# Zero matmuls on TensorE ahead of the first slabs, and the second chunk's split two squares earlier

## The chip, the cores and the metric

One core of a Trainium2 chip runs the whole kernel. Its engines work side by side, each through its own queue in order: TensorE (PE: matmuls and transposes; PEld is its weight load), VectorE (DVE), ScalarE (ACT), GpSimd (POOL) and SyncE (SP, which here issues nearly all transfers). The metric is the device time of one execution in microseconds (us), lower is better.

## What is computed

One layer of a diffusion model's trunk on 1024 tokens of width 1024, with 256 context tokens. Cut to what matters here:

```python
m = silu(cond) @ w_ada + b_ada                 # cond: c for x, c_ctx for ctx
shift, scale, gate = split(m, 3)
h  = rmsnorm(x, norm_g) * (1 + scale) + shift  # (1024, 1024); likewise hc from ctx
q, k, v, za, u, bg, cg, zc = split(h @ w_in)   # w_in: 1024 x 4096
attn = neighbourhood_attention(...) * silu(za)
conv = bg * conv3(cg * u) * silu(zc)
out  = x + gate * (concat(attn, conv) @ w_out)
```

All of it is float32. The large matmuls get that precision from operands split in two: a high part rounded to TensorE's faster format (fp32r), and a low part, the rest. Three products (high·high, high·low, low·high) make one.

## The kernel before

The change lies in the first 35 us, the opening of the kernel. There, h has to be made before the projections can run, and it is made in column blocks k = 0 to 7 of 128 channels, each in two halves (512 tokens each): `turn(half, k)` writes the high part `hh[k]` and the low part `hl[k]` from transposed tiles of x.

What is needed for that, by the names in the code (line numbers are those of the kernel before):

- **Slabs.** `load_slab(m, j)` fetches 256 columns of `w_ada`, for shift (j = 0) or scale (j = 1), 1024 KB each; (0, 0) and (0, 1) come in two halves of 512 KB. `products(m, j)` (line 594) multiplies them on TensorE by the two conditioning vectors `c2` (silu of c and c_ctx); `row_copy(m)` takes the result out of PSUM on ScalarE, and `modulation(m, rw)` turns it into columns with eight small matmuls, and adds bias and norm gain on VectorE (tile `ab`). m = 0 serves k = 0 and 1, m = 1 serves k = 2 and 3, and so on.
- **x.** Eight tiles of 128 tokens, `xx[0]` to `xx[7]`, 512 KB each. For tile n, `square(xx[n], n)` sums its squares on ScalarE, `root(n)` adds epsilon on VectorE and takes the power -0.5 on GpSimd, and `norm(xx[n], n)` scales the tile on VectorE. `transposed(half, k)` then transposes the four tiles of a half on TensorE, and `turn` applies `ab`: the high part on ScalarE, the same value in float32 on VectorE or ScalarE, and the difference on VectorE.
- **Chunks.** `chunk_load(CU, k)` fetches three blocks of 128 columns of `w_in` for channels k (192 KB, tile `wr`); `split_chunk(k)` makes `wh` on ScalarE and then `wl` on VectorE. `first_columns(half, k)` (line 670) is nine matmuls of 512 columns into the six accumulators `acc0`: three with `wh` and the high part of h, three with `wl` and the high part, three with `wh` and the low part.

Loads are issued on SP in the order slabs (0, 0) and (0, 1); x's tiles 0 to 3; chunk 0; x's tiles 4 to 7; chunk 1; slabs (1, 0) and (1, 1); chunks 2 and 3; slab (2, 0). Later slabs wait for the tile of an earlier one to come free.

The order of all this is written out by hand. The class `ordered` (line 44) chains the instructions of each engine in the order in which the program text emits them, so what stands first in the text runs first on its engine, and an instruction that waits holds up all behind it on the same engine. The text of the opening is:

```python
 718    products(0, 0)
 ...
 742    first_columns(0, 0)
 743    square(xx[6], 6)
 744    norm(xx[5], 5)
 745    root(6)
 746    square(xx[7], 7)
 747    norm(xx[6], 6)
 748    root(7)
 749    split_chunk(1)
 750    norm(xx[7], 7)
 751    first_columns(0, 1)
 752    products(1, 0, range(4))
 753    transposed(1, 0)
 754    turn(1, 0, act)
 755    products(1, 0, range(4, KT))
```

Before line 718, and ahead of everything else on TensorE, stands one transpose that brings the small vectors (c, c_ctx, norm gain, biases) into columns (`pv`, line 561). After the opening come the projections to q, k, v (with their own norms and rotations), the attention over 32 quarter heads with the gate and convolution projections as fillers, and the output projection.

Nearly every instruction goes through one helper line, so the profile shows L55 for most of them; they are told apart by tile names. In the profile, `tr` is the PSUM tile of transposes, products and modulation, `acc` the accumulators of first_columns, `c` the tile of `c2`, `xss` the sums of squares, `sqj` the squares.

Of the kernel before, what the change touches and what calls it, by code (L numbers as in the profile page):

```python
# [12 lines left out]
BF16 = mybir.dt.bfloat16  # L13
# [6 lines left out]
P = 128  # L20
# [19 lines left out]
def body(tc, es, x, ctxt, w_ada, b_ada, w_in, q_g, k_g, rpbr, w_out, vecs, cst, out):  # L40
# [21 lines left out]
    pe, act, dve, pool = every = [ordered(e) for e in (nc.tensor, nc.scalar, nc.vector, nc.gpsimd)]  # L62
    sp = ordered(nc.sync)

    def sbuf(name, side=None, bufs=1):
        kw = {} if side is None else {"side": side}
        return tc.tile_pool(name=name, bufs=bufs, reuse_waits="tile", **kw)
# [83 lines left out]
    cvp = hs.enter_context(sbuf("cvp", side="right"))  # L151
# [14 lines left out]
    def chunk_split(raw):  # L166
        raw = raw[:].rearrange("p a b -> p (a b)")
        wh = wpp.tile([P, 384], F32R, name="wh", tag="wh", bufs=12)
        wl = wpp.tile([P, 384], F32R, name="wl", tag="wl", bufs=12)
        act.copy(wh, raw)  # L170
        dve.tensor_tensor(wl, raw, wh[:].bitcast(F32), ALU.subtract)
        return wh, wl
# [348 lines left out]
    def tr():  # L521
        return ps0.tile([P, 512], F32, name="tr", tag="tr", bufs=2)

    strict[:] = every + [sp]
    xx, slabs, highs, lows, chunks, mods, pts = {}, {}, {}, {}, {}, {}, {}
# [31 lines left out]
    acc0 = [{}, {}, {}]  # L557
    for u, half in (0, 0), (2, 0), (0, 1), (2, 1), (1, 0), (1, 1):
        acc0[u][half] = ps0.tile([P, 512], F32, name=f"acc{u}{half}", tag=f"acc{u}{half}")

    pv = tr()
    pe.transpose(pv[:, :nvec], vec[:nvec], ident[:nvec, :nvec])
    dve.tensor_copy(vecT, pv[:, :nvec])
# [1 line left out]
    dve.tensor_scalar(b1, bsc, 1.0, None, ALU.add)  # L565
    c4 = cp.tile([P, KT, 4], F32R, name="c4")
    act.copy(c4[:, :, 0:2], c2)
    dve.tensor_tensor(c4[:, :, 2:4], c2, c4[:, :, 0:2].bitcast(F32), ALU.subtract)

    sums = {}  # L570

    def square(xtile, n):

        sqj = cvp.tile([P, D], BF16, name="sqj", tag="cu", bufs=1)
        sums[n] = xp.tile([P, 1], F32, name="xss", tag="xss", bufs=4)
        act.activation(sqj, xtile, AF.Square, scale=1.0 / 32, accum_out=sums[n])

    def root(n):
        dve.tensor_scalar(sums[n], sums[n], EPS, None, ALU.add)
        pool.tensor_tensor(sums[n], sums[n], mhalf[:, 0:1], ALU.pow)  # L580

    def norm(xtile, n):
        dve.tensor_scalar(xtile, xtile, sums[n], None, ALU.mult)
# [67 lines left out]
    def turn(half, k, on):  # L651

        modulated(rows_of(hh[k], half), rows_of(hl[k], half),
                  pts.pop((half, k))[:].rearrange("p (r b c) -> p r b c", r=8, b=8), k, 0, on)
# [15 lines left out]
    def first_columns(half, k, part=range(3)):  # L670

        wh, wl = chunks[k]
        h_, l_ = (v.rearrange("p (b r c) -> p b (r c)", b=8, r=16)[:, :, 64 * half:64 * half + 64]
                  for v in (hh[k], hl[k]))
        for i in part:
            for u in (0, 2, 1):
                uc = slice(u * P, (u + 1) * P)
                pe.matmul(acc0[u][half], (wl if i == 1 else wh)[:, uc], l_ if i == 2 else h_,
                          start=k == 0 and i == 0, stop=k == KT - 1 and i == 2)
# [33 lines left out]
    def split_chunk(k):  # L713
        chunks[k] = chunk_split(chunks[k])
# [25 lines left out]
    root(5)  # L740
    turn(0, 1, dve)
    first_columns(0, 0)
    square(xx[6], 6)
    norm(xx[5], 5)
    root(6)
    square(xx[7], 7)
    norm(xx[6], 6)
    root(7)
    split_chunk(1)
    norm(xx[7], 7)  # L750
    first_columns(0, 1)
    products(1, 0, range(4))
# [670 lines left out]
```

## Time and profile before

| | before |
|---|---|
| median of 3 runs | 651.97 us |
| lowest to highest | 651.77 to 652.3 us |
| profiled execution, its own time | 651.68 us |
| its span, first to last instruction | 649.9 us |
| mean granted TensorE clock | 0.994 |
| TensorE busy | 629.0 us (97%) |
| transferred | 125.46 MB |

The span is shorter than the execution's own time by 1.78 us that lie around it. A busy TensorE in the profile is not one at its peak: the ends of its pipelined matmuls are modelled. The granted clock is a share of full speed.

### The profile page before, as it was taken

To read this page: it belongs to the slowest core of one execution; us is meant where nothing else is said; L and a number is where in the kernel's file an instruction comes from. 1 tells how busy PE (TensorE), PEld (TensorE's weight loads), DVE (VectorE), ACT (ScalarE), POOL (GpSimd) and SP (SyncE) were. 2 spreads that over 40 slices of the span, in tenths; PEclk is the share of its full clock that TensorE was granted. 3 is DMA by queue.
4 is the path that set the end of the run, shared out by engine and by line. 5 is a ranking of instruction groups with operands and counts; after the bars stand their busy time and mean duration, and the time that the engine had idled before them with its cause. 6 is when DMAs were issued, how large, how long until landed. Compare 5 with 4: busy or idle time off the path is not lost.

```text
span 649.9 us, 10273 instructions
## 1 busy us (share of the span) xinstructions
PE 629.0 (97%) x3469; PEld 539.2 (83%) x3469; DVE 431.9 (66%) x814; ACT 322.6 (50%) x693; POOL 129.4 (20%) x137
## 2 busy tenths in 40 slices
PE   5799999999999999999999999999999999999997
PEld 1467799899899999977877888888888888888885
DVE  1557774966684856457786889988998864575111
ACT  3466653442553635428677558565685645352000
POOL 1203203312222132101121111111211111004321
PEclk9799999999999999999999999999999999999999
DMA  8854637686686898789939576886782223966521
GB/s 321 314 179 166 168 105 243 202 263 196 196 278 177 251 262 254 187 228 218 241 103 238 145 179 191 211 213 153 207 190 75 74 75 118 324 222 222 178 102 50
DMA packets 118864, 125.46 MB, mean 193 GB/s; under 512 B 32817, under 2 KB 89353, under 8 KB 117532
## 3 DMA queue, kind: packets, MB, share of 16 engines
q1 hardware_dynamic: 112348, 113.23, 60.9%
q10 hardware_dynamic: 6208, 11.05, 5.3%
q0 software_dynamic: 256, 0.54, 0.3%
q8 instruction: 27, 0.44, 0.3%
q14 instruction: 25, 0.20, 0.1%
HBM read 88.01 MB, written 38.53 MB: 195 GB/s over the span
## 4 chain that ended last, share of the span: by engine, by line
PE 72%; DMA 7%; DVE 7%; ACT 5%; SPq 4%; issue 2%; POOL 1%; ACTq 0%; DVEq 0%; POOLq 0%
PE pu L55 22%; PE pacc L55 17%; PE po L55 5%; PE pout L74 4%; PE pout L75 4%; PE pout L76 4%; SPq L55 3%; PE tr L55 3%; PE cacc L55 3%; PE pss L55 2%; PE pmx L55 2%; DMA v<-v_d 2%; DMA k_s<-k_d 2%; PE pc L55 2%; DVE mx L55 2%
## 5 line engine op out<-in xcount | busy, mean ns | idle before, releaser
L55 PE MATMUL pu<-h,uh 128*128 128x512 f32 x544 | 169.0, 392 | 0.0
L55 PE MATMUL pacc<-wh,h 128*128 128x384 f32 x512 | 135.1, 338 | 0.0
L55 PEld LDWEIGHTS pu<-h,uh 128*128 128x128 f32 x544 | 98.2, 188 | 17.0
L55 PE MATMUL pu<-h,ul 128*128 128x512 f32 x272 | 106.3, 391 | 0.0
L55 PEld LDWEIGHTS pacc<-wh,h 128*128 128x128 f32 x512 | 92.9, 188 | 0.1
L55 POOL TENSOR_TENSOR plc<-sc,phc 128x512 fp32r<-128x512 f32 x32 | 42.5, 1328 | 221.9 <-ACT sc L55 113.2
L55 PE MATMUL pacc<-wl,h 128*128 128x384 f32 x256 | 85.6, 335 | 0.0
L55 POOL TENSOR_TENSOR ss<-ss,few 128x4 f32<-128x4 f32 (+1 forms) x40 | 42.0, 1051 | 126.9 <-DVE ss L55 126.5
L55 PEld LDWEIGHTS pu<-h,ul 128*128 128x128 f32 x272 | 51.1, 188 | 11.2
L55 DVE TENSOR_TENSOR mx<-mx,sb 128x384 f32<-128x384 f32 (+1 forms) x64 | 55.1, 869 | 2.0
L75 PE MATMUL pout<-wol,yh 128*128 128x512 f32 x128 | 49.8, 389 | 0.0
L76 PE MATMUL pout<-woh,yl 128*128 128x512 f32 x128 | 49.6, 389 | 0.0
L74 PE MATMUL pout<-woh,yh 128*128 128x512 f32 x128 | 48.3, 389 | 0.0
L55 PEld LDWEIGHTS pacc<-wl,h 128*128 128x128 f32 x256 | 48.1, 188 | 0.1
L55 DVE TENSOR_REDUCE ss<-sq 128x4 f32<-128x260 f32 (+1 forms) x40 | 15.7, 393 | 46.0 <-ACT sq L55 45.0
L55 ACT COPY mg<-pmx 128x256 f32<-128x256 f32 x32 | 12.0, 374 | 57.8 <-PE pmx L55 47.2
L55 ACT ACTIVATE sq<-pacc 128x256 f32<-128x256 f32 x32 | 12.3, 386 | 53.1 <-PE pacc L55 52.3
L1355 DVE TENSOR_TENSOR ot<-pout,gate 128x512 f32<-128x512 f32 x16 | 10.8, 688 | 40.2 <-PE pout L76 37.7
L55 DVE TENSOR_TENSOR pll<-sb,phl 128x768 fp32r<-128x768 f32 (+2 forms) x33 | 29.3, 889 | 7.9 <-ACT sb L55 7.9
L1356 POOL TENSOR_TENSOR ot<-ot,xr 128x512 f32<-128x512 f32 x15 | 19.6, 1315 | 68.6 <-DVE ot L1355 67.6
L55 DVE TENSOR_TENSOR sc<-sc,mg 128x512 f32<-128x512 f32 x32 | 21.8, 683 | 17.1 <-ACT mg L55 17.1
L55 ACT ACTIVATE qn<-pacc,ss 128x64 f32<-128x64 f32 x128 | 30.1, 330 | 6.0 <-POOL ss L55 3.2
(146 smaller groups left out, 1276.0 us busy)
## 6 DMA issues: line engine op xcount, KB each, us to landing
uraw<-in_w_in SPq DMA_DIRECT2D x34, 256.0 KB
q_d<-qs SPq DMA_DIRECT2D x64, 128.0 KB
k_s<-k_d SPq DMA_DIRECT2D x16, 512.0 KB
q_s<-q_d SPq DMA_DIRECT2D x32, 256.0 KB
wr<-in_w_in SPq DMA_DIRECT2D x40, 192.0 KB
slab<-in_w_ada SPq DMA_DIRECT2D x6, 1024.0 KB
t_d<-btw SPq DMA_DIRECT2D x8, 576.0 KB
bt<-t_d SPq DMA_DIRECT2D x8, 576.0 KB
```

The costliest lines, as they stand in the source:

```text
L55: i = emit(*a, **kw)
L74: i = pe.matmul(ps, ah, bh, start=first, stop=False)
L75: pe.matmul(ps, ah, bl, start=False, stop=False)
L76: pe.matmul(ps, al, bh, start=False, stop=last)
L1355: dve.tensor_tensor(ot, ps, gate[:, cols], ALU.mult)
L1356: (dve if (nh, t) == (1, NB - 1) else pool).tensor_tensor(ot, ot, xr, ALU.add)
```

## The change

Two edits. The first fills a tile `warm` (128 x 512, bf16) with zeros on GpSimd, and puts 13 matmuls of it with itself on TensorE: six ahead of the vectors' transpose, seven between that and the first products. They write into the accumulator `acc0[2][1]`, which first_columns(1, 0) later starts anew. The tile takes a place in the ring of two buffers "ub", whose next user is `row_copy`. The second edit moves `split_chunk(1)` ahead of `norm(xx[5])`, of the squares 6 and 7, and of what belongs to them. No result changes.

```diff
     for u, half in (0, 0), (2, 0), (0, 1), (2, 1), (1, 0), (1, 1):
         acc0[u][half] = ps0.tile([P, 512], F32, name=f"acc{u}{half}", tag=f"acc{u}{half}")
 
+    warm = cvp.tile([P, 512], BF16, name="warm", tag="ub", bufs=2)
+    pool.memset(warm, 0.0)
+
+    def keep_clock(n):
+
+        for _ in range(n):
+            pe.matmul(acc0[2][1], warm[:, :P], warm, start=True, stop=True)
+
+    keep_clock(6)
     pv = tr()
     pe.transpose(pv[:, :nvec], vec[:nvec], ident[:nvec, :nvec])
     dve.tensor_copy(vecT, pv[:, :nvec])
...
     c4 = cp.tile([P, KT, 4], F32R, name="c4")
     act.copy(c4[:, :, 0:2], c2)
+    keep_clock(7)
     dve.tensor_tensor(c4[:, :, 2:4], c2, c4[:, :, 0:2].bitcast(F32), ALU.subtract)
...
     first_columns(0, 0)
+    split_chunk(1)
+    norm(xx[5], 5)
     square(xx[6], 6)
-    norm(xx[5], 5)
     root(6)
     square(xx[7], 7)
     norm(xx[6], 6)
     root(7)
-    split_chunk(1)
     norm(xx[7], 7)
     first_columns(0, 1)
```

## The prediction

> **What bounds the kernel now.** First the page's totals: TensorE fills nearly the whole span.
>
> ```profile
> span 649.9 us, 10273 instructions
> PE 629.0 (97%) x3469; PEld 539.2 (83%) x3469; DVE 431.9 (66%) x814; ACT 322.6 (50%) x693; POOL 129.4 (20%) x137
> ```
>
> So 20.9 us are left without a TensorE record. Next the table by stretches (columns: the stretch; its length; busy time of PE, PEld, DVE, ACT, POOL; granted clock; DMA share; GB/s). It shows that TensorE has no room from 36 us on (43.65 of 44), and that the transfers have run dry just before that (32 GB/s): what is ordered up to there is on chip by then.
>
> ```profile
> 30.50:36.00 5.50, 5.50 (x28) 2.28 (x27) 1.16 (x2) 2.98 (x5) 0.00 (x0) 1.00 0.12 32
> 36.00:80.00 44.00, 43.65 (x255) 33.80 (x254) 30.77 (x48) 28.50 (x45) 9.08 (x11) 1.00 0.58 185
> ```
>
> The change lies ahead of 36 us, so the question is how much sooner TensorE reaches that full stretch. Third, the chain of waits over the first 80 us (start, length, what), a few of its pieces:
>
> ```profile
> 5.27 8.58 DMA xx<-in_x
> ...
> 16.81 1.06 PE tr L55 x8
> ...
> 26.80 2.70 PE acc L55 x6
> 29.50 8.87 PE tr L55 x40
> ...
> 68.22 5.27 DMA wr<-in_w_in
> ```
>
> The chain runs through x's transfers and squares up to the modulation (16.81), through VectorE to the wl matmuls of first_columns(0, 1) (26.80), and from there along TensorE. Fourth, TensorE alone in five stretches of 3.4 us (length, PE busy, granted clock, DMA share, GB/s):
>
> ```profile
> 13.50:16.90 3.40, 1.64 (x9) 1.00 1.05 407
> 16.90:20.30 3.40, 2.20 (x16) 0.99 1.03 400
> 20.30:23.70 3.40, 3.38 (x8) 0.50 1.09 385
> 23.70:27.10 3.40, 1.78 (x6) 1.00 1.11 372
> 27.10:30.50 3.40, 3.40 (x9) 0.50 0.74 263
> ```
>
> The clock falls to half at 20.3, returns at 23.7, falls again at 27.1 and returns at 30.5. A sparse stretch is followed by one at 0.50, a full one by one at 1.00. Fifth, the instructions of TensorE, in order of time (start, length, engine, line, operation, out<-in, count, idle time before it and its releaser):
>
> ```profile
> 6.02 9.03 PE L55 MATMUL tr<-slab,c 128*2 128x256 f32 x32 [2.44 <-DMA slab<-in_w_ada]
> ...
> 19.12 0.77 PE L55 MATMUL tr<-ci,xx 128*128 128x128 f32 x5 [0.79 <-DVE xss L55]
> 20.32 1.65 PE L55 MATMUL acc<-h,wh 128*128 128x512 f32 x3 [0.43 <-ACT h L55]
> ...
> 23.04 1.15 PE L55 MATMUL acc<-h,wh 128*128 128x512 f32 x3
> 24.64 0.98 PE L55 MATMUL acc<-h,wh 128*128 128x512 f32 x3 [0.45 <-ACT wh L55]
> 26.80 1.42 PE L55 MATMUL acc<-h,wl 128*128 128x512 f32 x3 [1.18 <-DVE wl L55]
> ...
> 29.43 2.40 PE L55 MATMUL tr<-slab,c 128*2 128x256 f32 x8
> 31.76 0.66 PE L55 MATMUL tr<-ci,xx 128*128 128x128 f32 x4
> 32.35 1.89 PE L55 MATMUL tr<-slab,c 128*2 128x256 f32 x8
> ```
>
> Here stand the two idle gaps that the second edit aims at: 0.45 us before 24.64 for chunk 1's high part, 1.18 before 26.80 for its low part. At half clock six matmuls take 29.43 − 26.80 = 2.63 us, 0.44 each; so 0.22 at full clock.
>
> **First edit: the zeros.** The fill of the zeroed tile is not in the trace; between the row of the gate's accumulator, twice the elements and four times the bytes, and nothing:
>
> ```profile
> L55 POOL MEMSET gacc<- 128x1024 f32 x1 | 1.0, 957 | 16.3 <-DVE cv L55 16.3
> ```
>
> By elements half, 0.5 us, on a queue that has nothing else to do until 12.8 (a square root for x). I put the first zero matmul at 1.5. Thirteen matmuls, 512 columns wide, at half clock are 13 × 0.44 = 5.7 us, with the transpose of the vectors between them: they end near 7.4, or 7.0 if the clock opens at 6.7 (the marks above, 3.4 apart, counted back). The products queued behind them start there, not at 6.02. At full clock the 32 products cost at most 4 × 1.89 = 7.6 us (the row at 32.35), against 9.03: though the clock record starts at 1.00, part of those 9.03 ran at half. They end near 14 instead of 15.05. This gains nothing on the path, since the copy of their result is queued on ScalarE behind the fourth square:
>
> ```profile
> 16.20 0.56 ACT L55 COPY rw<-tr 2x512 f32<-2x512 f32 x1
> 17.02 1.06 ACT L55 ACTIVATE sqj<-xx 128x1024 bf16<-128x1024 f32 x1 [0.26 <-DMA xx<-in_x]
> ...
> 21.20 0.77 ACT L55 ACTIVATE h<-tr,ab 128x512 fp32r<-128x512 f32 x1
> 24.10 0.49 ACT L55 CAST wh<-wr 128x384 fp32r<-128x384 f32 x1
> 32.46 0.78 ACT L55 ACTIVATE h<-tr,ab 128x512 fp32r<-128x512 f32 x1 [7.87 <-PE tr L55]
> ```
>
> The copy starts at 16.20 either way; were this cover gone the edit would be worth about 1 us. But it has a price: with the products done near 14, the stretch 13.5 to 16.9 is busy for 0.5 instead of 1.64, and I expect 0.50 already from 16.9. Then the modulation's eight tiny matmuls (1.06 us) and the last transposes before first_columns(0, 0) run slow, and both are on the path (norm(xx[3]) stands behind the modulation on VectorE, the last transpose of the tile behind that norm). From below 0. From above double: 1.06 for the eight and about 0.35 for the transpose (half the 0.77 row), together 1.4. Between the ends the nearest row is that of the products' weight loads, the smallest against the largest:
>
> ```profile
> L55 PEld LDWEIGHTS tr<-slab,c x64: 80/85/129, 6.0 to 37.8; 128*2 128x2 f32 x64
> ```
>
> 129 to 85 is 1.5 to 1; 1.5 on the eight gives 0.55, and with the transpose's 0.35 it is **0.9 us lost**.
>
> [...] The stretch 23.7:27.1, with 1.78 of 3.40 busy and 0.50 after it, speaks for the loss.
>
> **Second edit: the split first.** On ScalarE wh of chunk 1 (0.49) now follows h(0, 1), which ends at 21.97: done near 22.5 instead of 24.59. Queued behind it are squares 6 and 7, each half a us later, and behind those two roots and two norms. VectorE's order:
>
> ```profile
> 18.31 0.75 DVE L55 TENSOR_SCALAR xx<-xx,xss 128x1024 f32<-128x1024 f32 x1
> ...
> 23.31 0.69 DVE L55 TENSOR_TENSOR h<-hw,h 128x512 fp32r<-128x512 f32 x1
> 23.92 0.75 DVE L55 TENSOR_SCALAR xx<-xx,xss 128x1024 f32<-128x1024 f32 x1
> ...
> 25.46 0.75 DVE L55 TENSOR_SCALAR xx<-xx,xss 128x1024 f32<-128x1024 f32 x1 [0.73 <-POOL xss L55]
> ...
> 26.20 0.55 DVE L55 TENSOR_TENSOR wl<-wr,wh 128x384 fp32r<-128x384 f32 x1
> 27.18 0.75 DVE L55 TENSOR_SCALAR xx<-xx,xss 128x1024 f32<-128x1024 f32 x1 [0.44 <-POOL xss L55]
> ```
>
> wl (0.55) moves from 26.20 to just behind the 23.31 row and ends near 24.55 instead of 26.75. Before, it lay inside VectorE's wait for GpSimd's root; now that wait is bare. So norm(xx[5]) moves by 0.55, and as its distance to norm(xx[7]) stays (the two roots between them still go through GpSimd), norm(xx[7]) ends at 27.93 + 0.55 = 28.48, with the 0.9 from above at 29.4.
>
> No DMA issue is moved past another one; SP's queue only reaches its later loads when TensorE frees their tiles. Is chunk 1 there at 22? Square 4 waited for x's fifth tile until 17.02; behind that in the queue stand three more tiles and the chunk,
>
> ```profile
> xx<-in_x SPq DMA_DIRECT2D x8, 512.0 KB
> wr<-in_w_in SPq DMA_DIRECT2D x8, 192.0 KB
> ```
>
> 3 × 512 + 192 KB = 1.77 MB, at about 0.4 MB per us 4.4 us: near 21.4. For certain only by 24.10. In between VectorE has no use for wh before 24.0, so lateness costs 0 to 0.6.
>
> TensorE: first_columns(0, 0) starts near 21.2, runs at half until 23.7 and ends near 24.4. first_columns(0, 1) then finds both parts (24.55 at first, 25.45 with the shift, where it waits a few tenths after three matmuls). Its nine at full clock are 2.0 us, done by 27.0 instead of 29.5. The eight products with slab (1, 0) add 1.89: 28.9. So what is late next is norm(xx[7]) at 29.4, not TensorE: the fourth transpose of (1, 0) waits for it, and h(1, 0) follows some 0.35 later (from below 0.3; from above the whole 0.70 between 31.76 and 32.46): 29.75 instead of 32.46. **The sum is 2.7 us.** With the bounds: nothing lost to the clock gives 3.6; 1.4 lost and 0.6 for the chunk give 1.6. From there the order of work is the old one, each step released by work on the chip, the loads of later slabs too, so I carry all 2.7 to the end.
>
> The profiled execution took 651.68 (span 649.9 and 1.78 around it): 651.68 − 2.7 = 648.98. The median, 651.97, is 0.29 above that execution, hence **649.3**.
>
> **Rivals.** (a) *The gain is given back later.* The chain still holds a transfer from 68.22 to 73.48. If that landing, or another, doesn't move, all behind it stays: 652.0. Against it: the DMA share of 0.12 before 36 us, so later loads start when released and meet no backlog. 0.09.
> (b) *The wait for norm(xx[7]) closes the clock.* TensorE is idle up to 0.5 us ahead of 29.4 and again around the transposes. If that is enough for one 3.4 us window at 0.50 where before there was 1.00, 1.7 us go: 650.9. Against: that stretch stays busy for some 2.8 of 3.4, and 1.78 was what closed it. 0.10. *Slower:* from the second such window on (two cost 3.4, three 5.1) the gain is outweighed: 652.7 to 654.4. 0.07.
> (c) *Zeros don't open the clock*, so the edit doesn't do what it says. The products start near 7.4 and run slow to about 10, as long as it took from 6.02 before: done near 15.5, still ahead of 16.20; and TensorE stays busy for long enough after 13.5 that the 0.9 isn't lost. 648.4, from the second edit alone. No row shows a zero operand. 0.06.
>
> **How the numbers follow.** Forecast 0.68, 648.4 to 650.4. A change under 0.2% (1.3 us) can't be told from none. Faster: 0.68, (c) 0.06 and a third of (b)'s first case, 0.77. Same: (a) and the rest of it, 0.16. Slower: 0.07. The range 647.9 to 651.2 holds the forecast with the runs' own scatter, (c) and (b)'s first case: 0.84.
>
> **What would show it.** Right: zero matmuls from about 1.5 to 7; the products at 0.22 each, done by 14.5; granted clock 0.50 from 16.9 to 23.7 and 1.00 after it; wh of chunk 1 directly behind h(0, 1); no idle time before the wl matmuls above 0.5 us; the fourth transpose of (1, 0) released by VectorE near 29.4; h(1, 0) near 29.75; and the same lead at 36 and 80 us. Wrong: a wait of wh for its transfer; 0.50 anywhere behind 27; or a lead at 36 us that is gone at 80.

## The result, and the profile after

In the comparison of the two kernels, 20 executions each, the median went from 651.1 to 648.6 us; the ratio is 0.997, with a 95% interval of 0.9956 to 0.9984. By that ratio the change takes 2.0 us less (1.0 to 2.9); the two medians lie 2.5 us apart. The forecast was 2.7 us, a ratio of 0.9959. The profiled execution of the changed kernel took 650.83 us. Its page begins:

```profile
span 649.0 us, 10300 instructions
PE 631.6 (97%) x3482; PEld 542.1 (84%) x3482; DVE 431.1 (66%) x814; ACT 322.6 (50%) x693; POOL 130.1 (20%) x138
```

TensorE in order of time, to be laid beside the prediction's fifth fence:

```profile
1.38 2.74 PE L55 MATMUL acc<-warm 128*128 128x512 bf16 x6 [1.38 <-POOL warm L55]
...
4.34 1.68 PE L55 MATMUL acc<-warm 128*128 128x512 bf16 x7
5.95 7.07 PE L55 MATMUL tr<-slab,c 128*2 128x256 f32 x32
16.27 1.05 PE L55 MATMUL tr<-ci,rw 2*128 2x2 f32 x8 [3.25 <-ACT rw L55]
...
18.59 1.33 PE L55 MATMUL tr<-ci,xx 128*128 128x128 f32 x5 [0.78 <-DVE xss L55]
19.93 1.65 PE L55 MATMUL acc<-h,wh 128*128 128x512 f32 x3
...
22.66 2.54 PE L55 MATMUL acc<-h,wh 128*128 128x512 f32 x6
25.04 0.85 PE L55 MATMUL acc<-h,wl 128*128 128x512 f32 x3
...
26.50 1.89 PE L55 MATMUL tr<-slab,c 128*2 128x256 f32 x8
28.31 0.66 PE L55 MATMUL tr<-ci,xx 128*128 128x128 f32 x4
```

Three things are to be seen. Six zero matmuls take 2.74 us, 0.46 each, the next seven only 1.68, 0.24 each: by that ratio zeros do open the clock, though its record reads 1.00 from the start. The products are done at 13.02 instead of 15.05, and then TensorE waits 3.25 us for ScalarE's `rw` where it waited 1.76: nothing of that is passed on. The row with that wait before, and two rows of ScalarE before that are needed below (the first square and h(0, 0)):

```profile
16.81 1.05 PE L55 MATMUL tr<-ci,rw 2*128 2x2 f32 x8 [1.76 <-ACT rw L55]
```

```profile
11.33 1.06 ACT L55 ACTIVATE sqj<-xx 128x1024 bf16<-128x1024 f32 x1 [7.01 <-DMA xx<-in_x]
...
19.49 0.78 ACT L55 ACTIVATE h<-tr,ab 128x512 fp32r<-128x512 f32 x1 [0.92 <-PE tr L55]
```

Third, from 19.93 to 28.31 no row has an idle time: both gaps ahead of `wh` and `wl` are gone. Granted clock in stretches of 3.4 us (length, PE busy, clock, DMA share, GB/s):

```profile
14.50:17.90 3.40, 1.53 (x11) 1.00 1.04 422
17.90:21.30 3.40, 2.70 (x8) 0.51 1.05 389
21.30:24.70 3.40, 3.40 (x9) 0.50 1.09 386
24.70:28.10 3.40, 3.40 (x16) 0.99 1.11 372
```

Before there were two half-clock stretches with an open one between, 20.3 to 23.7 and 27.1 to 30.5; now they are one, 18.0 to 24.8, of the same total length. On ScalarE (the first square, `wh` of chunk 1, h(1, 0)) and VectorE (`wl` of chunk 1, norm(xx[7])):

```profile
10.80 1.06 ACT L55 ACTIVATE sqj<-xx 128x1024 bf16<-128x1024 f32 x1 [5.66 <-DMA xx<-in_x]
...
21.48 0.51 ACT L55 CAST wh<-wr 128x384 fp32r<-128x384 f32 x1
...
29.01 0.78 ACT L55 ACTIVATE h<-tr,ab 128x512 fp32r<-128x512 f32 x1 [4.79 <-PE tr L55]
```

```profile
23.54 0.55 DVE L55 TENSOR_TENSOR wl<-wr,wh 128x384 fp32r<-128x384 f32 x1
...
27.09 0.75 DVE L55 TENSOR_SCALAR xx<-xx,xss 128x1024 f32<-128x1024 f32 x1 [0.73 <-POOL xss L55]
```

h(1, 0) starts at 29.01 instead of 32.46. But x arrived sooner in this execution: the first square started at 10.80, not 11.33. So the yardstick below is the distance from the first square to h(1, 0): 21.13 us before, 18.21 after. The edits' own lead is **2.92 us**. The two gaps were 1.63 us of that. For most of the rest there is an estimate: from first_columns(0, 0) on, TensorE spent 6.8 us at half clock before and 4.9 us here (19.93 to 24.8), and half of the difference is about 1.0.

At the end of this execution only 0.9 of span is left of it. The loss has a place. The chain of waits, first of before, then of the changed kernel, names two loads of attention's operands:

```profile
310.85 11.32 DMA v<-v_d
341.56 10.84 DMA k_s<-k_d
```

```profile
307.54 10.82 DMA v<-v_d
338.61 11.54 DMA k_s<-k_d
```

Their landings (start and length added) are 322.17 against 318.36, a lead of 3.81, and 352.40 against 350.15, a lead of 2.25. Behind the second landing, in one and the same stretch of before and then of after:

```profile
355.60:359.60 4.00, 3.80 (x22) 1.00 0.35 98
```

```profile
355.60:359.60 4.00, 3.92 (x18) 0.57 0.31 89
```

The changed kernel runs there mostly at half clock; of the 2.25, 0.9 are left at the end. Whether this belongs to the change is asked in the last experiment.

### The profile page after: what moved, and what is told of

Read it like the earlier page. It is cut to its first block, busy times and chain, and to the rows that moved or that the text cites. A ratio compares the mean times of both kernels' runs of the same rounds, so it can differ in the third digit from the quotient of the medians.

```text
span 649.0 us, 10300 instructions
## 1 busy us (share of the span) xinstructions
PE 631.6 (97%) x3482; PEld 542.1 (84%) x3482; DVE 431.1 (66%) x814; ACT 322.6 (50%) x693; POOL 130.1 (20%) x138
## 4 chain that ended last, share of the span: by engine, by line
PE 71%; DMA 9%; DVE 7%; ACT 5%; SPq 4%; issue 2%; POOL 1%; ACTq 0%; DVEq 0%
PE pu L55 20%; PE pacc L55 17%; PE po L55 5%; PE pout L76 4%; PE pout L75 4%; PE pout L74 4%; DMA k_s<-k_d 3%; SPq L55 3%; PE tr L55 3%; PE cacc L55 3%; PE pss L55 2%; PE acc L55 2%; PE pmx L55 2%; DVE mx L55 2%; DMA v<-v_d 2%
## 5 line engine op out<-in xcount | busy, mean ns | idle before, releaser
L55 DVE TENSOR_TENSOR sc<-sc,mg 128x512 f32<-128x512 f32 x32 | 21.8, 682 | 18.4 <-ACT mg L55 18.4
```

The source lines that it names most:

```text
L55: i = emit(*a, **kw)
```

## The experiments

Each further kernel has one profiled execution and 10 or 12 timed ones, against the kernel before on the same chip. A copy of the kernel before, timed like this, shows what such a ratio is worth:

| kernel | first square to h(1, 0), us | clock at half in the opening, us | h(1, 0) to the end, us | ratio to before, 95% |
|---|---|---|---|---|
| before | 21.13 | 20.3 to 23.7, 27.1 to 30.5 | 617.4 | |
| the change | 18.21 | 18.0 to 24.8 | 620.0 | 0.997 (0.9956 to 0.9984) |
| split_only | 17.39 | 19.2 to 22.6 | 618.6 | 0.9965 (0.9939 to 0.999) |
| zeros_only | 20.54 | 15.9 to 26.1 | 617.3 | 0.9992 (0.9968 to 1.0017) |
| bridge | 17.38 | none | 619.1 | 0.9965 (0.994 to 0.9989) |
| norms_first | 17.86 | 16.8 to 23.6 | 616.7 | 0.9949 (0.9929 to 0.9969) |
| bridge_norms | 17.28 | none | 619.0 | 0.9975 (0.9954 to 0.9997) |
| split_norms | 17.85 | 18.8 to 25.6 | 618.6 | 0.9963 (0.9943 to 0.9983) |
| after_a | 18.32 | 18.8 to 25.6 | 617.6 | 0.9971 (0.9947 to 0.9995) |
| after_b | 18.28 | 17.4 to 24.2 | 618.4 | 0.9958 (0.9933 to 0.9983) |
| before_a | 19.66 | 18.4 to 25.2 | 616.8 | 0.9961 (0.9934 to 0.9988) |
| before_b | 21.00 | 19.8 to 23.2, 26.6 to 30.0 | 619.1 | 0.9995 (0.9967 to 1.0024) |

before_a is the kernel before, and its interval leaves out 1. So single ratios of this table don't rank kernels that differ by less than about 0.4%. The change's own 0.997 is no further from 1 than that, so it needs support: in the last session of runs, 51 executions of the kernel before have a median of 651.27 us and 20 of the change 649.18, 2.1 us less (1.7 less than the 20 executions of before_a and before_b alone). What follows rests on the traces, and on ratios only where several agree.

**Each edit alone.** split_only is the kernel before with the diff's second edit, zeros_only with its first:

```diff
 # split_only
     first_columns(0, 0)
+    split_chunk(1)
+    norm(xx[5], 5)
     square(xx[6], 6)
-    norm(xx[5], 5)
...
-    split_chunk(1)
 # zeros_only
...
+    keep_clock(6)
     pv = tr()
...
+    keep_clock(7)
```

> The second edit alone, no zero matmuls. Theory S (the earlier split carries the gain, the zeros lie beside x's transfers): h(1, 0) starts 2.6 to 3.6 us sooner after the first square than before (before: 32.46 - 11.33 = 21.1 us; here 17.5 to 18.5), and the ratio to the kernel before is that of the change, 0.997 within 0.002. Rival Z (the zeros carry it, by moving the stretches of half clock): at most half of the lead is left, 19.3 us or more from first square to h(1, 0), ratio 0.9985 or above.

> The first edit alone, the split where it was. Theory S: products done near 13 us, but the modulation starts at the same distance from the fourth square; from first square to h(1, 0) 21.1 us, later by up to 0.9 if the clock closes ahead of the modulation; ratio 1.000 to 1.002. Rival Z: 19.5 us or less, ratio 0.998 or below.

With the split alone, h(1, 0) comes 17.39 us after the first square, a little better than the expected 17.5 to 18.5. The order of VectorE, TensorE and ScalarE at that point:

```profile
27.66 0.75 DVE L55 TENSOR_SCALAR xx<-xx,xss 128x1024 f32<-128x1024 f32 x1 [0.73 <-POOL xss L55]
```

```profile
26.32 1.89 PE L55 MATMUL tr<-slab,c 128*2 128x256 f32 x8
28.13 0.66 PE L55 MATMUL tr<-ci,xx 128*128 128x128 f32 x4
```

```profile
11.44 1.06 ACT L55 ACTIVATE sqj<-xx 128x1024 bf16<-128x1024 f32 x1 [7.17 <-DMA xx<-in_x]
...
28.83 0.78 ACT L55 ACTIVATE h<-tr,ab 128x512 fp32r<-128x512 f32 x1 [4.04 <-PE tr L55]
```

The norm ends at 28.41, TensorE is through with the products before that, and h(1, 0) follows 0.42 behind the norm. This one profile is 0.8 to 0.9 us shorter than the three of the change (18.21, 18.32, 18.28); its half clock lasts 3.4 us where theirs last 6.8, and one profile doesn't show whether the zeros cost that.

With the zeros alone, TensorE's modulation takes 1.86 us, not 1.05, and the old wait is still there:

```profile
16.78 1.86 PE L55 MATMUL tr<-ci,rw 2*128 2x2 f32 x8 [3.16 <-ACT rw L55]
...
27.73 0.96 PE L55 MATMUL acc<-h,wl 128*128 128x512 f32 x3 [0.97 <-DVE wl L55]
```

```profile
11.30 1.06 ACT L55 ACTIVATE sqj<-xx 128x1024 bf16<-128x1024 f32 x1 [6.16 <-DMA xx<-in_x]
...
20.43 0.78 ACT L55 ACTIVATE h<-tr,ab 128x512 fp32r<-128x512 f32 x1 [1.87 <-PE tr L55]
...
31.84 0.78 ACT L55 ACTIVATE h<-tr,ab 128x512 fp32r<-128x512 f32 x1 [6.31 <-PE tr L55]
```

From first square to h(0, 0) it needs 9.13 us, against 8.16 before (19.49 − 11.33): 0.97 lost, the price of a clock that closes ahead of the modulation. It makes that up behind it, where the clock stays open from 26.1, and ends at 20.54, between the two theories' numbers (21.1 and 19.5) and between the kernel before's own profiles (19.66 to 21.13). So theory S's number is missed by 0.6 us, but what it claims holds: the split carries the lead, and no gain of the zeros shows.

**What holds the opening now.** bridge adds zero matmuls to the change wherever TensorE idles; norms_first reorders VectorE instead:

```diff
 # bridge
     products(0, 1)
+    keep_clock(13)
...
     norm(xx[3], 3)
-    transposed(0, 0)
+    keep_clock(2)
+    transposed(0, 0, range(3))
+    keep_clock(3)
+    transposed(0, 0, [3])
     transposed(0, 1)
+    keep_clock(2)
 # norms_first
     first_columns(0, 0)
-    split_chunk(1)
-    norm(xx[5], 5)
...
+    act.copy(wh1, raw1)
     square(xx[6], 6)
     root(6)
+    dve.tensor_tensor(wl1, raw1, wh1[:].bitcast(F32), ALU.subtract)
...
+    norm(xx[5], 5)
     square(xx[7], 7)
+    root(7)
     norm(xx[6], 6)
-    root(7)
     norm(xx[7], 7)
-    first_columns(0, 1)
+    first_columns(0, 1, (0, 2, 1))
```

> The change, and 20 more zero matmuls in TensorE's idle stretches: 13 behind the first products, 2 behind the modulation, 3 ahead of the last transpose of the tile (0, 0), 2 ahead of first_columns(0, 0). If 0.22 us each and no later step held up, granted clock 1.00 from 4 to 30 us. Theory N (behind TensorE's half clock norm(xx[7]) stands close): first_columns is done some 3 us sooner, but the transposes of (1, 0) then wait for norm(xx[7]), so that h(1, 0) starts only about 0.4 us sooner after the first square than in the change (there 29.01 - 10.80 = 18.2 us): 17.8. Rival T (the half clock is all that holds the opening): 16.0 us or less.

> The change, with root(6) ahead of wl on VectorE, root(7) ahead of norm(xx[6]), and the low-part matmuls of first_columns(0, 1) last, so that norm(xx[7]) does not wait for GpSimd: it should end about 1.3 us sooner. Theory N (TensorE at half clock comes last in the change): h(1, 0) starts at most 0.2 us sooner after the first square than in the change, 18.0 us or more, unless the clock opens earlier than in the change's profile. Rival V (VectorE's chain to norm(xx[7]) comes last): 17.0 us.

bridge keeps the clock at 1.00 throughout the opening. TensorE now waits for `wl`, and after that for norm(xx[7]):

```profile
24.30 0.96 PE L55 MATMUL acc<-h,wl 128*128 128x512 f32 x3 [0.98 <-DVE wl L55]
...
25.89 1.89 PE L55 MATMUL tr<-slab,c 128*2 128x256 f32 x8
```

```profile
27.25 0.75 DVE L55 TENSOR_SCALAR xx<-xx,xss 128x1024 f32<-128x1024 f32 x1 [0.73 <-POOL xss L55]
```

The norm ends at 28.00, the products near 27.8, and h(1, 0) starts at 28.42, 17.38 us behind the first square: 0.8 sooner than in the change, where theory N said 0.4 and rival T 2.2 or more. In norms_first the wait for the first of the two roots is gone (norm(xx[6]) has no idle time before it, where the change has 0.73), and the wait for the second, ahead of norm(xx[7]), is 0.44 instead of 0.73; yet TensorE comes last:

```profile
27.45 0.75 DVE L55 TENSOR_SCALAR xx<-xx,xss 128x1024 f32<-128x1024 f32 x1 [0.44 <-POOL xss L55]
```

```profile
26.70 1.89 PE L55 MATMUL tr<-slab,c 128*2 128x256 f32 x8
28.52 0.66 PE L55 MATMUL tr<-ci,xx 128*128 128x128 f32 x4
```

The norm ends at 28.20, TensorE's transposes start at 28.52, and the distance is 17.86, 0.35 better than the change, not the 1.2 of rival V. (Its clock closed ahead of the modulation, at 16.8, and opened at 23.6, ahead of the change's; theory N had excepted that. That early closing also delayed VectorE: norm(xx[7]) ended 16.85 us after the first square, against 17.04 in the change, not the expected 1.3 sooner.) In these profiles each of the two is held by the other.

**Both at once, and no zeros at all.** bridge_norms joins the two edits above; split_norms puts the order of norms_first into the kernel before.

> The change with both additions: the 20 zero matmuls that keep the clock open, and the order of roots, norms and low-part matmuls that lets norm(xx[7]) end sooner. Theory N (two things stand close together ahead of the transposes of (1, 0): TensorE at half clock and norm(xx[7]); either alone gives only the distance to the other): from first square to h(1, 0) 16.2 to 16.7 us, against 17.4 with the zeros alone and 17.9 with the order alone; ratio to the kernel before about 0.9935. Rival W (something else, wl or a slab, holds it there): 17.2 us or more, ratio no lower than 0.995.

> The split first and the new order of roots and norms, with no zero matmuls at all. Theory S (the zeros of the change give nothing to the end): from first square to h(1, 0) 17.0 to 17.9 us, TensorE behind a half clock of one 3.4 us stretch coming last, and a ratio as that of the same order with the zeros, 0.995 within 0.002. Rival Z (the zeros are needed for the gain): 18.5 us or more, ratio 0.9975 or above.

bridge_norms missed: 17.28 us, not 16.2 to 16.7, and a ratio of 0.9975, not 0.9935. Something else holds it, as rival W had it, though neither of W's two:

```profile
16.88 1.05 PE L55 MATMUL tr<-ci,rw 2*128 2x2 f32 x8
...
24.17 0.98 PE L55 MATMUL acc<-h,wh 128*128 128x512 f32 x3 [0.52 <-DVE h L55]
...
25.77 1.89 PE L55 MATMUL tr<-slab,c 128*2 128x256 f32 x8
```

TensorE waits 0.52 us for the low part of h(0, 1) on VectorE; six matmuls and eight products later it is 27.6. And the modulation has no idle time in its row: the 13 zeros ahead of it, begun later in this execution, were still running when `rw` was there. split_norms reached 17.85 us and a ratio of 0.9963 with no zero matmul in it, as theory S expected, though its half clock lasted 6.8 us (18.8 to 25.6) where S had 3.4; its x arrived 1.3 us later than before's (first square at 12.61), so its span says little.

**The same kernels again.** after_a and after_b are the change, before_a and before_b the kernel before, unaltered. What they decide between is read from the time from h(1, 0) to the last instruction, 620.0 us in the first profile of the change and 617.4 in that of before. Theory P is that each execution has its own times of half clock and that this rest scatters alike in both kernels; the author's estimate for it, from those two profiles, was 616.5 to 619 us, with no half clock near 355 us. Rival G is that the changed kernel gives part of the lead back, every time.

> The changed kernel again, unaltered, for a second profile. [...] Rival G (the kernel gives part of the lead back later, every time): 619.5 or more.

> The changed kernel a third time, as above: theory P 616.5 to 619 us from h(1, 0) to the end, rival G 619.5 or more.

> The kernel before again, unaltered. Theory P: from first square to h(1, 0) 20 to 22 us, by where the half clock falls (the first profile had 21.1, with the clock closed from 20.3 to 23.7 and from 27.1 to 30.5), and from h(1, 0) to the end 616.5 to 619 us. Rival G: 617.4 within 0.5.

> The kernel before a third time, as above: theory P 616.5 to 619 us from h(1, 0) to the end, rival G 617.4 within 0.5.

The clock closed and opened at 18.8 and 25.6 us in after_a and at 17.4 and 24.2 in after_b, not at 18.0 and 24.8 again, as theory P said. From h(1, 0) to the end the changed kernel took 617.6 and 618.4 us, not 619.5 or more: rival G falls, and neither profile has a half clock near 355 us. The first profile's loss there is that execution's own. The kernel before had 616.8 and 619.1, so this rest scatters by over 2 us whatever the opening did (before_b a tenth beyond theory P's bound). In the mean of three profiles it is 617.8 before and 618.7 after; three don't tell 0.9 us from the scatter, so a small part given back stays open. The opening of before scatters too. In before_a the clock fell once, not twice:

```profile
18.40:21.80 3.40, 2.60 (x9) 0.51 1.06 383
21.80:25.20 3.40, 3.28 (x9) 0.50 1.09 386
25.20:28.60 3.40, 2.36 (x9) 0.99 1.11 372
```

Its distance is 19.66 us, below theory P's 20 to 22. Over three profiles each, the means are 20.60 before and 18.27 after: a lead of 2.3 us, which agrees with the 2.0 of the timed runs.

## Why the prediction was right, point by point

- **The zeros' own cost.** The fill took 0.53 us (POOL's row of it), the first zero matmul started at 1.38: as worked out. In the first profile the zero matmuls took 0.46 us each up to 4.1 and 0.24 each from 4.34 on, by which the clock opened near 4.3, not 6.7; the products started at 5.95 with no delay and were done at 13.0, not 14. In after_a they started at 6.30 and in after_b at 7.33, and were done at 13.4 and 14.4: the forecast is one of the cases that occur. That they gain nothing behind the fourth square held.
- **The 0.9 lost to an early closing.** It exists, and is well sized in sum: 0.97 in zeros_only, 0.96 in norms_first (from first square to h(0, 0), 20.47 − 11.35 = 9.12 against 8.16). Its terms were off in opposite directions: in zeros_only the modulation took 0.81 longer (1.86 against 1.05), not 0.55, and the rest 0.16, not 0.35. But it isn't there in every execution. In the change's first profile the modulation still took 1.05 us and the loss was 0.14 (19.10 − 10.80 = 8.30); after_a has 8.32, and only after_b, with 9.12, lost 0.96. The step failed where it read the marks of one execution as those of the next: the same instructions saw the clock close at 15.9, 16.8, 17.4, 18.0 and 18.8 us. What a stretch must lack for the clock to close was an estimate from single rows too. It need not be without work: the stretch 23.7 to 27.1 of the kernel before had 1.78 of 3.40 busy on matmuls of 512 columns, and 0.50 after it. The stretch 14.5 to 17.9 of the change, with 1.53 busy and 0.51 after it, says less: all that ran there were the modulation's two-column matmuls and three transposes, and no run shows what these alone do to the clock.
- **norm(xx[7]) as what is late next.** True in one of the change's three profiles. In after_b, where the 0.9 was lost, the norm ended at 30.00, TensorE had come to the transposes at 29.72, and h(1, 0) followed at 30.43. In the first profile the norm ended at 27.84 and TensorE came to the transposes only at 28.31; in after_a it was 28.42 and 28.99. In the first profile TensorE was where the sum had it (28.9, less the 0.53 by which x was sooner), but the norm was 1.0 sooner than told (29.4, less 0.53), because the 0.9 was hardly lost. So it is partly luck that the sum came near, 2.7 forecast and 2.92 in this profile: with 0.14 lost instead of 0.9 the sum would have been 3.5, and TensorE, 0.5 behind the norm, hid most of the mistake. In split_only and bridge the norm is the last, as told. The bound of 3.6 for a clock that costs nothing on the way is what split_only has: 21.13 − 17.39 = 3.74.
- **Chunk 1 in time.** `wh` started at 21.48 directly behind h(0, 1), with no wait.
- **All of it carried to the end.** True up to the load of v near 310 us (a lead of 3.81, 0.53 of it x's); behind that, the scatter between executions, 2 us and more, is as large as the gain. Rival (a) did not occur in the change: its transfer ran from 64.75 to 70.04, where before it ran from 68.22 to 73.49, so the opening's 3.45 came through whole. The transfer isn't always the same, though: the chain of waits of norms_first and that of bridge have it as

```profile
64.96 5.27 DMA wr<-in_w_in
```

```profile
64.15 6.93 DMA wr<-in_w_in
```

  and in bridge 1.7 us of the opening's lead go there. bridge_norms has 6.73. Why these two take longer stays open.
- **Rivals (b) and (c).** In no profile with the split first did the clock close again in the opening once it had opened, so (b) is out where it was put; once it did fall later, to 0.57 in the mean of 355.6 to 359.6 us, in the first profile of the change. (c) is out: behind the zeros the 32 products took 7.07 us, in the change as in after_a, zeros_only, bridge and norms_first; without zeros they took 9.03 in before and 8.61 in split_only.

Part of the gain's size rests on something the prediction did not know: the second half-clock stretch of the kernel before (27.1 to 30.5) is not a fixed cost. Measured against before_a, where it is missing, the mean of the change's three profiles leads by 1.4 us (19.66 − 18.27) rather than 2.9; there the idle time ahead of the wl matmuls is 1.04 us, and ahead of the wh matmuls there is none. So the term that was oversized is the lead itself, taken from one execution of before.

## What to carry to other kernels

Look for a short operation that stands behind a longer one which nobody needs yet: ordering `wh` and `wl` ahead of two squares cost half a microsecond on a chain that had slack until then, and took idle time off the busiest engine: 1.6 us, 1.0 and 1.9 in the three profiles of the kernel before. Before the clock is kept open with zeros, ask whether the work that runs at half clock comes last. Here the result of the warmed products had to wait behind x's squares in any case, and in the sparse time behind them the clock closed again, at 15.9 to 18.8 us; and bridge, with 33 zero matmuls and an open clock, needs as long as split_only with none (17.38 and 17.39 us). And a sum made from one profile should treat the times at which the clock changes as unknown: take the cost with and without each half-clock stretch as bounds.

## What the runs showed of the hardware that was not expected

- The time at which the clock closes and opens differs between executions of the same instructions. With the zeros at the head, the same seven zero matmuls took 1.68 us in the first profile of the changed kernel, 2.03 in after_a and 2.77 in norms_first. The distances between the marks stay at multiples of about 3.4 us (before 3.4; the change 6.8; zeros_only 10.2).
- Busy time in the records doesn't decide it alone: a stretch with 1.64 of 3.40 busy left the clock open in the kernel before (13.5 to 16.9, with 0.99 behind it), one with 2.20 closed it (16.9 to 20.3, with 0.50 behind it), where all that ran were eight matmuls two columns wide and eight transposes. So the prediction's "a sparse stretch is followed by one at 0.50" had its exception in its own first row. Nor did more busy time always go with an open clock: 2.36 of 3.40 busy left an open clock open (25.2 to 28.6 in before_a), 2.60 and 2.70 left a closed one closed (18.4 to 21.8 there, 17.9 to 21.3 in the change).
- Executions of one kernel differ by 0.8%, more than the change's effect: the kernel before ran from 648.23 to 653.66 us in the first comparison.
